# Modulation granules earlier in the weight stream of a two-layer hybrid decoder trunk

## The chip, the cores and the metric

One core of a Trainium2 chip. The metric is the device time of one execution in microseconds (us). The kernel before takes 1177.0 us, the median of three runs from 1176.92 to 1178.7. PE is TensorE, DVE is VectorE, ACT is ScalarE, POOL is GpSimd and SP is SyncE, which issues the loads.

## The reference

Two layers over one sequence of 256 rows and 1024 channels, all in float32. Each layer has three parts: a SwiGLU network (FFN1), token mixing, and another SwiGLU network (FFN2). Each part starts with a normalisation whose scale and shift, and ends with a residual whose gate, come from a vector c through a 1024 x 9216 matrix per layer:

```python
def modulate(x, g, shift, scale):
    return rmsnorm(x, g) * (1 + scale[:, None, :]) + shift[:, None, :]

c_act = jax.nn.silu(c)
for l in range(DEPTH):
    mod = c_act @ w_ada[l] + b_ada[l]
    sh1, sc1, gt1, sh2, sc2, gt2, sh3, sc3, gt3 = jnp.split(mod, N_MOD, axis=-1)
    h = modulate(x, ln_ffn1_g[l], sh1, sc1)
    x = x + 0.5 * gt1[:, None, :] * swiglu(h, ffn1_w_gate[l], ffn1_w_up[l], ffn1_w_down[l])
    h = modulate(x, ln_mix_g[l], sh2, sc2)
    x = x + gt2[:, None, :] * token_mixing(h, w_in[l], ...)
    h = modulate(x, ln_ffn2_g[l], sh3, sc3)
    x = x + 0.5 * gt3[:, None, :] * swiglu(h, ffn2_w_gate[l], ffn2_w_up[l], ffn2_w_down[l])
return rmsnorm(x, final_g)
```

Token mixing projects h once and feeds three groups of heads: a convolution of 31 taps with a normalisation over channels, block-sparse attention, and a gated delta rule. Their outputs go through one output projection.

## The kernel before, in words

The activations stay on the chip, transposed: xT has 128 partitions, 8 channel blocks and 256 sequence columns. All weights, 252.9 MB of them, are read once from DRAM, in granules of 1 MB (256 columns or 256 rows of a matrix), into a ring of four tiles `raw` (N_RAW = 4). SP issues a granule when the one four places before it has been released, that is, when every unit cut from it has been read. The order of the granules is the list `seq`, written by `plan_ffn` and `plan_mix` before any instruction is.

A weight unit is 128 output columns of all 1024 channels. It is split in two parts for TensorE: ACT writes the rounded part `hi`, then DVE writes the rest `lo` (POOL in the opening, where `cfg["lo_first"]` says "gp"). The activations are split in the same way, and PE adds three products for each of 8 blocks, hi by hi, hi by lo and lo by hi, so 24 products of 256 columns per unit. Six converted units can be waiting (N_UNIT = 6).

A modulation vector v of layer l (0 shift, 1 scale, 2 gate of FFN1; 3 to 5 of mixing; 6 to 8 of FFN2) takes four granules of `w_ada` (`adaunit`). DVE multiplies the rows of each granule by the partition's element of c_act and adds them up, two operations per granule (`ada_step`), in a tile of 128 x 1024 called `Lb` or `adaacc`. `extract` then turns this tile with PE, four transposes at a time into `px`, and sums each turned block with a reduction on DVE into the columns of `mod`; `complete` adds the bias. Biases, gains and convolution taps are loaded as rows (`rowsA`, `rowsB`) and turned into columns by `columns(l, part)`: part 0 the biases, part 1 the other rows, and rowsB, which holds the convolution taps.

The table `ADA` says which vectors are loaded during which part: in layer 0 vectors 2 to 5 in FFN1, 6 and 7 in mixing; in layer 1 vector 7 alone in mixing. `plan_ffn` spreads them over the slots of its loop over pairs of units (`extra`). `plan_mix` places a granule behind every fourth converted unit, counting from the second, and puts those that remain behind the last granule of `w_out`.

The opening: scale (vector 1 of layer 0) is loaded first and summed while ACT and PE make the sums of squares. With scale known, xT times scale is split in S-hi (tiles S6a, Q) and S-lo (S3a, V, v), and six units are multiplied with it, without shift. Shift (vector 0) is loaded behind the second gate granule. When its sum is there, `columns(0, 1)` and the extraction follow, and the part that shift adds to the six units is made by 96 row products (`sh_b`), turned at the end (`turn_row`) and used as a bias. The following units use H, the full modulated input. At the starts of the other parts the shift instead stands in two more columns of S6a to v, so that products of 258 columns bring its part along.

In mixing the order of instructions comes from a planner: the class `Clock` keeps an estimated time for each engine, and the code asks it before it converts a unit (`pump`), extracts a vector, or gives a convolution tap to DVE (`cacc` from `hc` and `colB`) or to ACT and POOL (`ctap`, then `cacc`). One recurrence on POOL inverts small matrices; its result goes through DRAM (`scr_w`) into `Wc`.

Of the kernel before, what the change touches and what calls it, by code (L numbers as in the profile page):

```python
# [11 lines left out]
F32R = mybir.dt.float32r  # L12
# [165 lines left out]
def trunk(ctx, tc, t, out):  # L178
# [121 lines left out]
    def plan_ffn(l, which, ada):  # L300
# [11 lines left out]
        start = 4 if key == ("f", 0, 1) else 0  # L312
# [8 lines left out]
        for q in range(FB // 2):  # L321
            for n, w in (("g", wg), ("u", wu)):
                g = kgran(w, 256 * q, 256)
                for j in range(2):
                    wunit(key + (n, 2 * q + j), g, kview(256, j))
                if key == ("f", 0, 1) and (q, n) == (1, "g"):
                    for i in range(4):
                        adaunit(0, 0, i)
            if q:
                extra(2 * q - 2)  # L330
                for j in range(2):
                    down(2 * q - 2 + j)
                extra(2 * q - 1)
# [4 lines left out]
    def plan_mix(l, ada):  # L338
# [5 lines left out]
        def unit(name, i, g, view, width=D):  # L344
# [4 lines left out]
            if todo and count[0] >= count[1]:  # L349
                adaunit(*todo.pop(0))  # L350
                count[1] += 4
# [57 lines left out]
    for i in range(4):  # L409
        adaunit(0, 1, i)  # L410
# [44 lines left out]
    def extract():  # L455
# [18 lines left out]
        if (l, v) == (1, 0):  # L474
            columns(l, 1)
# [3 lines left out]

    def ada_step(item):  # L480
        _, (l, v), g, i, _ = item
        raw = grans[g]["tile"].rearrange("p (k n) -> p k n", n=D)
        if i == 0:
# [185 lines left out]
    def begin(gs, sh):  # L669
# [4 lines left out]
        if sh is not None:  # L674
# [3 lines left out]
        return dict(gs=gs, sh=sh, parts=[(a[:, :S1 if sh is not None else S], b[:, :S1 if sh is not None else S])  # L678
                                         for a, b in zip(his, los)])
# [95 lines left out]


    scr_g = nc.dram_tensor("scr_g", [D], F32, kind="Internal").ap()

    def ffn(l, which, G, normed, gate_v, nxt):
# [4 lines left out]
        def act_fn(f, o):  # L784
            if bias and f < 4:
                s = normed_out(o[:, 0])
                act.activation(s, s, AF.Silu, bias=bias[2 + f])
            else:
                s = sb([128, S], "tmp2", bufs=4)
                act.activation(s, o[:, 0], AF.Silu)  # L790
# [107 lines left out]
        def first():  # L898
            keys = [key + (n, i) for n in "gu" for i in range(2)]
            if G["sh"] is not None:  # L900
                cols = [sb([128, 2], f"bias{i}") for i in range(2)]
                outs = [bank((128, S1)) for _ in range(2)] + [ps([128, S1], f"a{i}") for i in range(2)]
                norm = {}
                first_units(keys, outs, G, lambda: norm.update(h=normed([pump] * 3)))
                for i in range(2):
                    for j in range(2):
                        dve.tensor_copy(cols[i][:, j:j + 1], outs[2 * j + i][:, S:S + 1])
            else:
                keys += [key + ("g", i) for i in (2, 3)]
                pair = [ps([128, 2, S], f"a{i}") for i in range(2)]  # L910
                raws.extend(bank() for _ in range(2))
                outs = [pair[i][:, j] for j in range(2) for i in range(2)] + [o[:, 0] for o in raws]
                for kk, o in zip(keys, outs):
                    low_last(o, need(kk), G["parts"])
                for k in range(KB):
                    act.activation(nscr["t"][:, k], xT[:, k], AF.Copy, scale=G["gs"][:, k:k + 1])
                    gp.tensor_tensor(nscr["t"][:, k], nscr["t"][:, k], nscr["r"], op=OP.mult)
                while (0, 0) not in ada_acc or not ada_wait:
                    step_stream()
                both = sb([128, KB, 2], "sh_b", F32R)  # L920
                p = [ps([2, n, 128], tag) for n, tag in ((4, "a2"), (2, "m0"))]
                job = ada_wait[0]
                columns(0, 1)
                keep_warm(3)
                for h in range(2):
                    extract()
                    c = slice(4 * h, 4 * h + 4)
                    act.copy(both[:, c, 0], job[3][:, c])
                    dve.tensor_tensor(both[:, c, 1], job[3][:, c], both[:, c, 0], op=OP.subtract)
                for h in range(2):  # L930
                    for i, kk in enumerate(keys):
                        for k in range(4 * h, 4 * h + 4):
                            for x, w in enumerate(conv[kk]):
                                mm(p[i // 4][:, i % 4], both[:, k], w[:, k], k == 0 and x == 0 and i % 4 == 0, (k, x) == (KB - 1, 1))
                row = sb([2, 6, 128], "Wc")
                early = {}

                def rows_out():
                    act.copy(row[:, 0:4], p[0])
                    act.copy(row[:, 4:6], p[1])  # L940

                norm = dict(h=normed([lambda: None] * 3 + [lambda: [done(kk, 1, True) for kk in keys[:2]]], True))
                rows_out()
                early.update((i, normed_out(outs[i])) for i in range(4))
                act.preload_act_table_set("silu_and_others")
                for i, kk in enumerate(keys[2:]):
                    done(kk, 2 * (i == 3), True)

                def turn_row():
                    p = ps([128, 6, 2], "a3")  # L950
# [1045 lines left out]
```

## Time and profile before

| | |
|---|---|
| median of three runs | 1177.0 us |
| profiled execution | 1178.1 us, span 1176.3 us |
| PE busy | 1103.2 us (94%) |
| DVE busy | 875.1 us (74%) |
| ACT busy | 597.3 us (51%) |
| POOL busy | 141.9 us (12%) |
| mean granted clock of PE | 0.978 |
| DMA | 256.52 MB, mean 218 GB/s |
| opening, up to the first down product of FFN1 | 0 to 70 us |
| FFN1, mixing, FFN2 of layer 0 | to about 235, 424 and 600 us |

The span runs from the first to the last instruction; the 1.8 us between it and the execution's own time lie around it. The kernel's instructions all go through one helper, so they carry the line L171, and groups are told apart by the tiles that they write and read. A row "out<-in" names them without buffer numbers. In a timeline the number in square brackets is how long the engine stood idle before the row, and behind the arrow is what ended it. Matmuls overlap one another, so the distance between starts says what one costs. An f32 product takes two rows; a split product (hi, lo) takes one.

### The profile page before, as it was taken

The numbers are of one execution on the slowest core, as the hardware profiler recorded it, in microseconds if no ns is written. First come the engines' busy times: TensorE is split into PE (matmuls) and PEld (weight loads), VectorE is DVE, ScalarE is ACT, GpSimd is POOL, SyncE is SP. The second block draws the span as 40 slices with busy tenths as digits, with TensorE's granted clock in tenths as the row PEclk, the third lists the DMA queues.
The fourth block names the chain that finished last, engine by engine and source line by source line (L and its number), as shares of the span: only waits on it lengthen the run. The fifth ranks groups of instructions, "written<-read, shape, count | busy, mean of one in ns | idle before, by whom it ended". The sixth has DMA issues, their size and how long they took to land.

```text
span 1176.3 us, 22000 instructions
## 1 busy us (share of the span) xinstructions
PE 1103.2 (94%) x9085; PEld 1037.8 (88%) x9085; DVE 875.1 (74%) x1350; ACT 597.3 (51%) x1011; POOL 141.9 (12%) x187
## 2 busy tenths in 40 slices
PE   5799999999969689999999999999996999999997
PEld 4799999968868689999999999997785899999996
DVE  5778778757977788867779887774877869766554
ACT  4364444448356464534456444444764676544443
POOL 0710000020650010000001000001037101000002
PEclk9899999999989999999999999999998999999999
DMA  9759798846423558968864997882562434876640
GB/s 327 251 171 345 282 335 279 265 123 198 125 100 131 186 173 298 329 237 318 287 228 159 333 331 254 306 287 80 166 202 75 145 102 157 310 239 216 208 132 36
DMA packets 167660, 256.52 MB, mean 218 GB/s; under 512 B 8272, under 2 KB 134056, under 8 KB 167560
## 3 DMA queue, kind: packets, MB, share of 16 engines
q1 hardware_dynamic: 166536, 252.95, 63.5%
q0 software_dynamic: 1024, 2.16, 0.8%
q8 instruction: 71, 1.16, 0.4%
q14 instruction: 29, 0.24, 0.1%
HBM read 252.86 MB, written 2.23 MB: 217 GB/s over the span
## 4 chain that ended last, share of the span: by engine, by line
PE 74%; DVE 10%; ACT 7%; POOL 4%; issue 2%; DMA 2%; SPq 0%; POOLq 0%; ACTq 0%; DVEq 0%
PE pm L171 45%; PE pa L171 26%; DVE adaacc L171 3%; PE px L171 2%; DVE lo L171 2%; ACT hi L171 1%; ACT tmp L171 1%; ACT L171 1%; POOL xin_LT L171 1%; DMA raw<-in_w_in_dram 1%; DVE S3a L171 1%; DVE mod L171 1%; POOL W L171 1%; DMA xin_LT<-in_x_dram 1%; DVE v L171 1%
## 5 line engine op out<-in xcount | busy, mean ns | idle before, releaser
L171 PE MATMUL pm<-H,hi 128*128 128x256 f32 x2816 | 510.0, 283 | 1.2 <-DVE H L171 1.2
L171 DVE TENSOR_TENSOR lo<-raw,hi 128x1024 fp32r<-128x1024 f32 (+1 forms) x300 | 361.3, 1227 | 110.9 <-ACT hi L171 110.4
L171 PEld LDWEIGHTS pm<-H,hi 128*128 128x128 f32 x2816 | 433.7, 190 | 4.3 <-DVE H L171 1.4
L171 ACT CAST hi<-raw 128x1024 fp32r<-128x1024 f32 (+1 forms) x306 | 311.5, 1042 | 193.1 <-PE pm L171 84.2
L171 PE MATMUL pm<-H,lo 128*128 128x256 f32 x1408 | 393.0, 281 | 0.0
L171 PEld LDWEIGHTS pm<-H,lo 128*128 128x128 f32 x1408 | 265.4, 189 | 0.0
L171 PE MATMUL pa<-Y,hi 128*128 128x256 f32 x1312 | 236.3, 283 | 3.7 <-DVE xT L171 3.7
L171 PEld LDWEIGHTS pa<-Y,hi 128*128 128x128 f32 x1312 | 202.6, 191 | 4.3 <-DVE xT L171 4.3
L171 PE MATMUL pa<-Y,lo 128*128 128x256 f32 x656 | 184.6, 281 | 0.0
L171 PEld LDWEIGHTS pa<-Y,lo 128*128 128x128 f32 x656 | 126.3, 193 | 0.0
L171 POOL TENSOR_TENSOR xin_LT<-xin_LT 128x256 f32<-128x256 f32 x35 | 27.2, 776 | 645.0 <-ACT xin_LT L171 642.7
L171 ACT CAST Y<-tmp 128x256 fp32r<-128x256 f32 x88 | 35.8, 406 | 120.4 <-DVE tmp L171 120.4
L171 DVE SCALAR_TENSOR_TENSOR adaacc<-raw,c_act,adaacc 128x1024 f32<-128x1024 f32 x70 | 93.9, 1342 | 1.6
L171 DVE SCALAR_TENSOR_TENSOR Lb<-raw,c_act,Lb 128x1024 f32<-128x1024 f32 x56 | 71.8, 1282 | 4.3 <-DMA raw<-in_w_ada_dram 3.0
L171 DVE TENSOR_TENSOR Y<-tmp,Y 128x256 fp32r<-128x256 f32 x88 | 37.4, 425 | 41.6 <-ACT Y L171 41.6
L171 PE MATMUL pm<-Y,raw 128*128 128x256 f32 x288 | 65.9, 382 | 0.0
L171 PEld LDWEIGHTS pm<-Y,raw 128*128 128x128 f32 x288 | 53.6, 190 | 7.5
L171 PE MATMUL pa<-hi,Y 128*128 128x512 f32 x176 | 54.8, 393 | 0.0
L171 ACT ACTIVATE tmp<-pm 128x256 f32<-128x256 f32 x78 | 29.6, 379 | 49.4 <-PE pm L171 49.3
L171 DVE TENSOR_REDUCE mod<-px 128x4 f32<-128x512 f32 x34 | 23.5, 690 | 38.5 <-PE px L171 38.4
L171 DVE SCALAR_TENSOR_TENSOR cacc<-hc,colB,cacc 128x256 f32<-128x256 f32 x92 | 44.7, 499 | 4.6 <-POOL cacc L171 3.1
L171 DVE TENSOR_TENSOR tmp<-tmp,pm 128x256 f32<-128x256 f32 x80 | 33.2, 415 | 12.1 <-ACT tmp L171 12.1
(302 smaller groups left out, 1278.3 us busy)
## 6 DMA issues: line engine op xcount, KB each, us to landing
raw<-in_w_ada_dram SPq DMA_DIRECT2D x70, 1024.0 KB
raw<-in_ffn_w_gate_dram SPq DMA_DIRECT2D x44, 1024.0 KB
raw<-in_ffn_w_up_dram SPq DMA_DIRECT2D x44, 1024.0 KB
raw<-in_ffn_w_down_dram SPq DMA_DIRECT2D x44, 1024.0 KB
raw<-in_w_in_dram SPq DMA_DIRECT2D x12, 1024.0 KB
raw<-in_w_in_dram SPq DMA_DIRECT2D x20, 512.0 KB
raw<-in_w_out_dram SPq DMA_DIRECT2D x16, 512.0 KB
raw<-in_w_in_dram SPq DMA_DIRECT2D x4, 768.0 KB
```

What stands on the lines that cost most here:

```text
L171: return getattr(real, op)(*args, **kw)
```

## The change

1. In the opening, the four granules of shift are loaded directly behind those of scale. DVE sums only the first half of the rows of each granule; the other half goes to PE as f32 products of c_act with the raw rows, 512 columns at a time, and two more products with ones add the 128 partial sums of DVE (`ada_rows`). Two copies, eight transposes of one column each and a copy give the vector. Four units are computed with 258 columns, instead of six without shift; the 96 row products, two groups of warming products and `turn_row` fall away. xT times scale times rstd (PT) is made by eight operations of DVE, before by ACT and POOL. POOL makes two lo, before six.
2. `plan_ffn` starts placing the modulation granules of the first FFN1 at slot 2, before at slot 4.
3. `plan_mix` places a modulation granule behind every second converted unit, before every fourth.
4. `columns(0, 1)`, which turns rowsB, comes behind the extraction of vector 2 in FFN1, before in the opening.

The core of the diff (three hunks that only rename or drop the old opening are cut):

```diff
-        start = 4 if key == ("f", 0, 1) else 0
+        start = 2 if key == ("f", 0, 1) else 0
...
-                if key == ("f", 0, 1) and (q, n) == (1, "g"):
-                    for i in range(4):
-                        adaunit(0, 0, i)
...
                 adaunit(*todo.pop(0))
-                count[1] += 4
+                count[1] += 2
...
-    for i in range(4):
-        adaunit(0, 1, i)
+    for v in (1, 0):
+        for i in range(4):
+            adaunit(0, v, i)
...
-        if (l, v) == (1, 0):
+        if (l, v) in ((0, 2), (1, 0)):
             columns(l, 1)
...
+    def ada_rows(raw, g, i):
+        if i == 0:
+            ada_acc[0, 0] = [ps([1, 512], f"a{2 + h}") for h in range(2)] + [sb([128, D], "adaacc")]
+        *rows, acc = ada_acc[0, 0]
+        halves = [slice(512 * h, 512 * h + 512) for h in range(2)]
+        for h in range(2):
+            mm(rows[h], c_act[:, 2 * i + 1:2 * i + 2], raw[:, 1, halves[h]], i == 0, False)
+        c = c_act[:, 2 * i:2 * i + 1]
+        if i == 0:
+            dve.tensor_scalar(acc, raw[:, 0], c, 0.0, op0=OP.mult, op1=OP.add)
+        else:
+            dve.scalar_tensor_tensor(acc, raw[:, 0], c, acc, op0=OP.mult, op1=OP.add)
+        release(g)
+        if i < 3:
+            return
+        row = sb([1, D], "Lb")
+        for h in range(2):
+            mm(rows[h], ones[:, 0:1], acc[:, halves[h]], False)
+            dve.tensor_copy(row[:, halves[h]], rows[h])
+        p = ps([128, KB], "x")
+        for k in range(KB):
+            pe.transpose(p[:, k:k + 1], row[:, 128 * k:128 * k + 128], ident[0:1, 0:1])
...
+    def first_serial(keys, outs, G, between):
+        for i, (key, o) in enumerate(zip(keys, outs)):
+            low_last(o, need(key), G["parts"], between if i == 0 else None)
...
     gs = need_mod(0, 1)
     G = begin(gs, None)
-    keep_warm(3)
+    rstd(sums)
     for k in range(KB):
         scaled_hi(G, k)
-        scaled_lo(G, k)
-    step_stream()
-    rstd(sums)
-    for _ in range(4):
+    for i in range(4):
+        step_stream()
+        for k in {1: range(4), 2: range(4, KB)}.get(i, ()):
+            scaled_lo(G, k)
+    cfg["lo_first"] = ["gp", "gp"]
+    G["sh"] = mods[0, 0]
+    for _ in range(2):
+        step_stream()
+    G["shift"](G["sh"])
+    for k in range(KB):
+        dve.scalar_tensor_tensor(nscr["t"][:, k], xT[:, k], gs[:, k:k + 1], nscr["r"], op0=OP.mult, op1=OP.mult)
+    for _ in range(2):
         step_stream()
```

The program of DVE in the opening, behind the scale of layer 0 (mod_174 is scale, mod_253 shift; `lo` are weight units), as it is now:

```order
L171 TENSOR_SCALAR adaacc<-raw,c_act 128x1024
L171 SCALAR_TENSOR_TENSOR adaacc<-raw,c_act,adaacc 128x1024
L171 SCALAR_TENSOR_TENSOR S3a<-xT,mod_174,S6a 128x256 x3
L171 SCALAR_TENSOR_TENSOR V<-xT,mod_174,S6a 128x256
L171 SCALAR_TENSOR_TENSOR adaacc<-raw,c_act,adaacc 128x1024
L171 SCALAR_TENSOR_TENSOR V<-xT,mod_174,S6a 128x256 x2
L171 SCALAR_TENSOR_TENSOR v<-xT,mod_174,Q_192 128x256 x2
L171 SCALAR_TENSOR_TENSOR adaacc<-raw,c_act,adaacc 128x1024
L171 COPY Lb<-pa_206 1x512
L171 COPY Lb<-pa_207 1x512
L171 COPY mod_253<-px 128x8
L171 TENSOR_TENSOR mod_253<-mod_253,colA 128x8
```

Before, the sum of shift (adaacc) stood behind all S-lo pieces and two lo, as one block of eight operations; now it is four operations, and the first units' shift columns follow directly.

SP's program at the end of mixing 0 (raw is the ring; `w_out` is the output projection's weight, `ffn_w_gate` the first of FFN2), before:

```order
L171 DMA raw<-in_w_in_dram 128x8x256
L171 DMA raw<-in_w_in_dram 128x8x128
L171 DMA raw<-in_w_in_dram 128x4x384 x2
L171 DMA raw<-in_w_ada_dram 128x2x1024
L171 DMA raw<-in_w_in_dram 128x8x256
L171 DMA raw<-in_w_in_dram 128x8x128
L171 DMA raw<-in_w_out_dram 128x1024 x8
L171 DMA raw<-in_w_ada_dram 128x2x1024 x5
L171 DMA raw<-in_ffn_w_gate_dram 128x8x256
```

and now:

```order
L171 DMA raw<-in_w_in_dram 128x4x384
L171 DMA raw<-in_w_ada_dram 128x2x1024
L171 DMA raw<-in_w_in_dram 128x4x384
L171 DMA raw<-in_w_ada_dram 128x2x1024
L171 DMA raw<-in_w_in_dram 128x8x256
L171 DMA raw<-in_w_ada_dram 128x2x1024
L171 DMA raw<-in_w_in_dram 128x8x128
L171 DMA raw<-in_w_out_dram 128x1024 x8
L171 DMA raw<-in_w_ada_dram 128x2x1024 x2
L171 DMA raw<-in_ffn_w_gate_dram 128x8x256
```

Five modulation granules stood between the last `w_out` and FFN2's first weight, now two; the other three stand among the granules of `w_in`. In layer 1 it was one and is none.

DVE's program in the same place (mod_4275 is vector 6, shift, and mod_4346 vector 7, scale, of FFN2; xT is the residual), before:

```order
L171 TENSOR_TENSOR lo<-raw,hi 128x1024 x2
L171 SCALAR_TENSOR_TENSOR adaacc<-raw,c_act,adaacc 128x1024 x2
L171 TENSOR_REDUCE mod_4275<-px 128x4 x2
L171 TENSOR_TENSOR mod_4275<-mod_4275,colA 128x8
L171 TENSOR_SCALAR adaacc<-raw,c_act 128x1024
L171 SCALAR_TENSOR_TENSOR adaacc<-raw,c_act,adaacc 128x1024 x7
L171 TENSOR_REDUCE mod_4346<-px 128x4 x2
L171 TENSOR_TENSOR mod_4346<-mod_4346,colA 128x8
L171 SCALAR_TENSOR_TENSOR mod_4346<-mod_4346,colA 128x8
L171 TENSOR_TENSOR sh_l<-mod_4275,sh_h 128x8
```

and now (mod_4272 is vector 7):

```order
L171 TENSOR_TENSOR lo<-raw,hi 128x1024 x2
L171 SCALAR_TENSOR_TENSOR adaacc<-raw,c_act,adaacc 128x1024 x4
L171 TENSOR_TENSOR lo<-raw,hi 128x1024 x3
L171 TENSOR_REDUCE mod_4272<-px 128x4 x2
L171 TENSOR_TENSOR mod_4272<-mod_4272,colA 128x8
L171 SCALAR_TENSOR_TENSOR mod_4272<-mod_4272,colA 128x8
L171 TENSOR_TENSOR sh_l<-mod_3349,sh_h 128x8
```

Vector 6 is finished earlier, inside mixing, and four operations of vector 7's sum are left where ten stood.

## Rows read from the trace of the kernel before

**Rows 1.** Page, part 1: engine, busy us (share of the span), instructions.
```profile
PE 1103.2 (94%) x9085; PEld 1037.8 (88%) x9085; DVE 875.1 (74%) x1350; ACT 597.3 (51%) x1011; POOL 141.9 (12%) x187
```

**Rows 2.** Waits of PE, 65 to 430 us: total, times, longest.
```profile
PE px L171 <- DVE adaacc L171: 8.4, 2, 4.8
PE pa L171 <- DMA Wc<-scr_w: 6.4, 1, 6.4
```

**Rows 3.** Timeline of PE, opening: start us, us, engine line op out<-in xcount [idle before <-releaser].
```profile
25.84 1.11 PE L171 MATMUL pa<-S6a,hi 128*128 128x256 f32 x6
...
43.83 0.23 PE L171 MATMUL px<-kc,rowsA 23*128 23x23 f32 x1
49.90 0.43 PE L171 MATMUL px<-kc,rowsB 98*128 98x98 f32 x1 [5.84 <-DVE colA L171]
...
70.33 0.40 PE L171 MATMUL pa<-Y,hi 128*128 128x256 f32 x2
```

**Rows 4.** Timeline of SyncE's queue, opening.
```profile
11.82 0.40 SPq L171 DMA_DIRECT2D raw<-in_ffn_w_gate_dram  x1
...
20.76 1.08 SPq L171 DMA_DIRECT2D raw<-in_w_ada_dram  x1
```

**Rows 5.** Timeline of DVE, opening.
```profile
24.88 1.27 DVE L171 SCALAR_TENSOR_TENSOR S3a<-xT,mod,S6a 128x256 fp32r<-128x256 f32 x3
...
36.42 13.33 DVE L171 SCALAR_TENSOR_TENSOR adaacc<-raw,c_act,adaacc 128x1024 f32<-128x1024 f32 x7
```

**Rows 6.** Windows: stretch, busy us of each engine (x), PEclk, DMA share, GB/s.
```profile
50.00:54.00 4.00, 4.00 (x13) 3.35 (x14) 0.43 (x2) 0.00 (x0) 1.02 (x2) 0.50 1.09 348
```

**Rows 7.** Timelines of ACT, DVE and POOL, opening.
```profile
20.24 1.04 ACT L171 CAST hi<-raw 128x1024 fp32r<-128x1024 f32 x1 [2.85 <-DMA raw<-in_ffn_w_gate_dram]
...
61.49 2.60 DVE L171 SCALAR_TENSOR_TENSOR H<-PT,mod,H 128x256 fp32r<-128x256 f32 x1
...
61.34 2.46 POOL L171 TENSOR_TENSOR lo<-raw,hi 128x1024 fp32r<-128x1024 f32 x1 [10.32 <-ACT hi L171]
```

**Rows 8.** Page, part 5: op out<-in xcount | busy, mean ns | idle before.
```profile
L171 PE MATMUL pm<-Y,raw 128*128 128x256 f32 x288 | 65.9, 382 | 0.0
```

**Rows 9.** Timeline of DVE, end of mixing 0.
```profile
386.87 0.69 DVE L171 TENSOR_TENSOR Y<-cacc,Y 128x512 fp32r<-128x512 f32 x1 [2.84 <-ACT Y L171]
...
395.54 2.60 DVE L171 SCALAR_TENSOR_TENSOR adaacc<-raw,c_act,adaacc 128x1024 f32<-128x1024 f32 x2
...
416.08 4.63 DVE L171 TENSOR_TENSOR lo<-raw,hi 128x1024 fp32r<-128x1024 f32 x4
```

**Rows 10.** Timeline of PE, end of mixing 0.
```profile
411.61 1.08 PE L171 MATMUL px<-kc,adaacc 128*128 128x128 f32 x4 [4.81 <-DVE adaacc L171]
...
424.23 0.28 PE L171 MATMUL pm<-S6a,hi 128*128 128x258 f32 x1
```

**Rows 11.** Timeline of PE, turns in FFN2 of layer 0.
```profile
523.48 0.29 PE L171 MATMUL px<-kc,rowsA 80*128 80x80 f32 x1 [0.79 <-DVE mod L171]
...
526.26 0.63 PE L171 MATMUL pm<-H,hi 128*128 128x256 f32 x2
```

**Rows 12.** Convolution tile cacc in mixing 0: duration ns min/median/max, first and last start.
```profile
L171 POOL TENSOR_TENSOR cacc<-cacc,ctap x14: 716/734/1536, 328.1 to 362.7; 128x256 f32<-128x256 f32 x14
```

**Rows 13.** Timeline of DVE, end of mixing 1.
```profile
957.62 0.69 DVE L171 TENSOR_TENSOR Y<-cacc,Y 128x512 fp32r<-128x512 f32 x1 [2.84 <-ACT Y L171]
```

**Rows 14.** Timeline of PE, end of mixing 1.
```profile
972.96 0.89 PE L171 MATMUL px<-kc,adaacc 128*128 128x128 f32 x4 [2.20 <-DVE mod L171]
973.50 0.78 PE L171 MATMUL pa<-Y,hi 128*128 128x256 f32 x2
...
980.35 0.40 PE L171 MATMUL pa<-Y,hi 128*128 128x256 f32 x2
980.70 0.28 PE L171 MATMUL pm<-S6a,hi 128*128 128x258 f32 x1
```

**Rows 15.** Waits of SyncE's queue, 65 to 395 us.
```profile
SPq L171 <- DVE adaacc L171: 26.7, 9, 11.8
```

More of the change, by code (lines that the diff above doesn't have):

```diff
@@ L482, in ada_step @@
         raw = grans[g]["tile"].rearrange("p (k n) -> p k n", n=D)
+        if (l, v) == (0, 0):
+            return ada_rows(raw, g, i)
         if i == 0:
@@ L673, in begin, with shift @@
         los = [pieces[2][:, k] for k in range(3)] + [pieces[3][:, k] for k in range(3)] + [pieces[4][:, k] for k in range(2)]
-        if sh is not None:
+        def shift(sh):
             hi, lo = split_col(sh)
@@ L677, in begin @@
                 dve.tensor_copy(pieces[piece][:, :, S:S1], src[:, k:k + n].unsqueeze(2).to_broadcast([128, n, S1 - S]))
-        return dict(gs=gs, sh=sh, parts=[(a[:, :S1 if sh is not None else S], b[:, :S1 if sh is not None else S])
-                                         for a, b in zip(his, los)])
+        if sh is not None:
+            shift(sh)
+        return dict(gs=gs, sh=sh, parts=list(zip(his, los)), shift=shift)
     def begin_whole(gs, sh, w):
@@ L899, in first @@
             keys = [key + (n, i) for n in "gu" for i in range(2)]
[L900 to L918, printed above, removed]
-                    step_stream()
[L920 to L923, printed above, removed]
-                keep_warm(3)
[L925 to L950, printed above, removed]
-                    for i in range(6):
-                        pe.transpose(p[:, i], row[:, i], ident[0:2, 0:2])
-                    b = sb([128, 6], "bias0")
-                    dve.tensor_reduce(b, p, axis=AX.X, op=OP.add)
-                    bias.extend(b[:, i:i + 1] for i in range(6))
-                    acc.extend(ps([128, 2, S], f"a{i}") for i in range(4))
-                    for i in range(2):
-                        first_act(i, early[i], early[2 + i], bias[i], bias[2 + i])
@@ L960, in first @@
-            if G["sh"] is not None:
-                su = [normed_out(o) for o in outs]
-                acc.extend(ps([128, 2, S], f"a{i}") for i in range(4))
-                for kk in keys:
-                    done(kk)
-                act.preload_act_table_set("silu_and_others")
-                for i in range(2):
-                    first_act(i, su[i], su[2 + i], cols[i][:, 0:1], cols[i][:, 1:2])
-                return norm["h"], None
-            return norm["h"], turn_row
-        bias, raws = [], []
@@ L972, in ffn @@
-        hparts, pending = first()
+            cols = [sb([128, 2], f"bias{i}") for i in range(2)]
+            outs = [bank((128, S1)) for _ in range(2)] + [ps([128, S1], f"a{i}") for i in range(2)]
+            norm = {}
+            opening = key == ("f", 0, 1)
+            (first_serial if opening else first_units)(keys, outs, G, lambda: norm.update(h=normed([pump] * 3, opening)))
+            for i in range(2):
+                for j in range(2):
+                    dve.tensor_copy(cols[i][:, j:j + 1], outs[2 * j + i][:, S:S + 1])
@@ L973, in ffn @@
+            su = [normed_out(o) for o in outs]
+            acc.extend(ps([128, 2, S], f"a{i}") for i in range(4))
+            for kk in keys:
+                done(kk)
+            act.preload_act_table_set("silu_and_others")
+            for i in range(2):
+                first_act(i, su[i], su[2 + i], cols[i][:, 0:1], cols[i][:, 1:2])
+            return norm["h"]
+        hparts = first()
         last = list(range(FB - 2 if nxt else FB - 3, FB))
```

28 lines of the change are left out of this document (10 added, 18 removed).

## Prediction

> **What bounds the kernel now.** The page comes first: TensorE (PE) is busy 1103.2 of 1176.3 us [rows 1], so time can only come out of PE's idle stretches or out of stretches where its clock is low. I then asked for PE's waits between 65 and 430 us, which is the rest of FFN1, the first mixing and its end. The largest entry is PE's transposes px waiting for the modulation sums adaacc of VectorE (DVE), 8.4 us in two waits; next come 6.4 us for Wc, the inverse that comes back through DRAM [rows 2]. Third, the timelines of the opening, because that is where PE idles longest. A reader should see there that the first unit starts at 25.84, that six units end at 43.83, that PE then waits 5.84 us for DVE, and that the first down product (the moment when four gate and four up units are done) comes at 70.33 [rows 3]. The wait is DVE's: the four granules of shift are issued behind three weight granules, the first of them at 20.76 [rows 4], and seven operations of their sum take 13.33 [rows 5], where one undisturbed pair takes 2.60 [rows 9]. Behind that wait PE's granted clock is 0.50, that is 1.2 GHz [rows 6]. Last, the two ends of mixing: layer 0 has five trailing modulation granules, layer 1 has one, and the same code otherwise. That comparison carries the largest term.
>
> Gains and losses are sums of differences against the profiled execution, 1178.1 us with its span of 1176.3. The median of the runs shown is 1177.0, so I take differences off that.
>
> **Opening.** The order moves shift's four granules into the ring places of gate, up, gate and the first modulation granule, issued from 11.82 to 20.76 [rows 4]. The first such place landed at 20.24 [rows 7], and at 348 GB/s [rows 6] one MB takes 3.0 us, so the four land at about 20.2, 23.2, 26.2 and 29.2. DVE is done with scale at 24.88, where its S-lo pieces begin [rows 5]; now four half sums stand among eight S-lo operations: 4 x 1.3 (half of the pair of 2.60) and 8 x 0.42 (three take 1.27) give 8.6, so the last half sum ends at 33.5. PE adds the other halves meanwhile; behind DVE remain two f32 products of 512 columns. The kernel has a measured row for f32 products of 256 columns, 65.9 us for 288 rows, two rows per product, so 0.46 each [rows 8]; 512 columns cost 0.92 and the two 1.8, double at the low clock. That makes 35.3. Copies, eight one-column transposes, the sum and the five shift columns follow. The nearest row is the extraction at the end of mixing, from px at 411.61 to the end of its shift columns at 416.08, 4.5 us with wider transposes and two reductions [rows 9, 10]; below it lies 1.5. I take 2.7, nearer the lower end because no reduction (0.69 each) is left. First unit: **38.0** instead of 25.84.
>
> From there PE has no 96 small row products, no warming products and no wait. Six units took 43.83 - 25.84 = 18.0, 3.00 each with the slow start in it [rows 3]. Eight units take 24.0; 1.0 more for the later weights, whose first granule is released by the first shift sum. So the first down product is at 63.0 instead of 70.33: **-7.3**. Best end: first unit at 36.5 and nothing lost behind, -9.8. Worst end: the last products at half clock (1.8) and one small DVE operation blocked by each of POOL's two lo, as one H was for 2.60 beside a lo of POOL [rows 7], where three S-lo pieces of the same size take 1.27 [rows 5]: -2.
>
> The turn of rowsB leaves the opening, where it lay inside the wait, and comes behind the extraction of gate in FFN1. The same three turns stand in FFN2 of layer 0: PE waits 0.79 before the first and then runs slow, two products in 0.63 [rows 11] where 0.40 is usual [rows 3]. Such a slow restart costs 1.6 at the end of mixing 1 (below). So the two turns cost between 0.8 and 2.4, and I take **+1.8**, since the idle time behind which PE restarts is nearly the same. The four vectors of FFN1 that start two slots earlier only spread the loads and sums; DVE has room there, so 0.
>
> **Mixing.** In layer 0 six granules instead of three are summed inside, in layer 1 four instead of three. Each is 2.6 us of DVE and one ring place. PE's idle time inside is set by chains through POOL and DRAM (Wc 6.4), not by DVE's total, and part of the added sum falls in that wait. Thirteen convolution taps move from DVE to POOL (9 and 4), 0.73 each [rows 12]. I take **+1**, between -1 and +8.
>
> The Trainium skill ("SBUF — State Buffer", section "Who interferes with whom") says that a DVE instruction with two SBUF inputs and a GpSimd instruction that reads SBUF exclude each other for a whole instruction. The H row above, 2.60 where a third of 1.27 is usual, agrees. By that rule the thirteen taps could block DVE for their whole length.
>
> **End of mixing 0.** I lay layer 1 over layer 0 by the same DVE row, Y<-cacc at 386.87 and at 957.62, a shift of 570.75 [rows 9, 13]. FFN2 starts at 424.23 in layer 0 and at 980.70 in layer 1 [rows 10, 14]; layer 0 is 424.23 + 570.75 - 980.70 = 14.3 us later, for four more trailing granules. With two left it is layer 1's end and one more pair of 2.60: 14.3 - 2.6 = **-11.7**. The lower bound is three pairs of DVE time, -7.8; the upper -13.
>
> **End of mixing 1.** With none trailing, the 2.20 us wait of px for mod [rows 14] goes, and so does the restart at low clock behind it. The 48 products left then, in 16 steps of three, take 7.2 us from 973.50 to 980.70, and at full clock a step takes 0.35 (980.35 to 980.70), 5.6 in all, so 1.6 goes: **-3.8**, between -2.2 and -4.6. Late next is the chain through the residual to FFN2's first product, which there starts without a wait.
>
> Sum: -7.3 + 1.8 + 1 - 11.7 - 3.8 = -20.0, so 1177.0 - 20.0 = **1157.0**.
>
> **Rivals.**
> - *Mixing gives it back.* The added sums lie on DVE's chain to scr_l and to the lo halves: four granules of 2.6 are 10.4 instead of +1: 1166.4. For it: DVE is busy 74% [rows 1]. Against: PE's large waits there name DMA, not DVE [rows 2]. Chance 0.13.
> - *POOL's taps block DVE.* Thirteen taps of 0.73 [rows 12] hold up two-input operations of DVE, cacc and lo, and PE behind them: 13 x 0.73 = 9.5 instead of +1, 1165.5. Against: fourteen taps in layer 0 at a median of 0.73 put no entry for themselves among PE's waits up to 430 [rows 2, 12]. Chance 0.07. This is the result of the rule named above.
> - *The opening gains nothing.* Four MB ahead of the weights make the first unit later than 45: 1164.3. For it: the four MB land one behind the other, 3.0 us each, before any weight. Chance 0.10.
> - *The trailing sums were not what held FFN2.* Only the DVE time of three pairs goes (-7.8) and mixing 1 gives 2.2: 1162.5. Chance 0.08.
> - *Slower: the ring stalls.* Four raw buffers; a granule of modulation holds one until DVE reaches it. SyncE's queue has waited 26.7 us in nine waits for adaacc, the longest 11.8 [rows 15]. If each of the four moved granules waits the longest and the following weights reach PE late by as much, 4 x 11.8 = 47.2: 1204. It decides from 20 us of new PE waits in mixing, 5 per granule. Against: these nine waits were there already, and none of PE's entries up to 430 names hi, lo or a granule [rows 2]. Chance 0.05.
> - *It does not do what it says*: the earlier places could be given back by the planner, so that the last sums again come behind the output projection. The order shows the trailing issues at two and none, so I leave this at no chance of its own.
>
> **How the numbers follow.** The forecast has 0.57: 1150 (all best ends: -9.8 + 0.8 - 1 - 13 - 4.6 = -27.6) to 1163. The range 1148 to 1168 takes in the next four cases. Outside lie the ring and sums of bad ends. About 0.2%, 2.4 us, is what a measurement of this kernel tells from no change. Slower by more than that: 0.05, the ring; within: 0.02, two bad cases at once; faster: 0.93.
>
> **What would show it.** Right: px<-adaacc gone from PE's waits up to 430 except about 1 us; first unit near 38 and first down product near 63; the distance from Y<-cacc to FFN2's first product falls from 37.4 to 25.7 in layer 0 and from 23.1 to 19.3 in layer 1; the distance from the first down product to Y<-cacc of layer 0 (316.5) longer by about 3. Wrong: a first unit behind 45, new PE waits for hi or lo in mixing, SyncE waits for adaacc above 12 us there, or taps of POOL as releasers of PE.

## The result and the profile after

The kernel after takes 1168.7 us (median of four runs, 1166.5 to 1171.2). The kernel before, run beside it, takes 1177.9. The ratio is 0.992 [0.990, 0.994], so 9.2 us are gained where 20.0 were forecast, and the forecast range ended just below, at 1168. The profiled execution of after took 1166.5 us, span 1164.7, and is the fastest of the four: the stages below add up to 11.6 us and not to 9.2.

The stages, from the starts of the same instructions in the two profiled executions (us):

| stage | before | after | difference | forecast |
|---|---|---|---|---|
| to the first down product | 70.3 | 62.1 | -8.3 | -7.3 |
| rest of FFN1, with the moved turn | 168.3 | 170.2 | +2.0 | +1.8 |
| mixing 0, to Y<-cacc | 148.3 | 151.3 | +3.0 | } +1 |
| mixing 1, to Y<-cacc | 148.6 | 149.3 | +0.7 | } |
| end of mixing 0 | 37.4 | 26.9 | -10.5 | -11.7 |
| end of mixing 1 | 23.1 | 18.5 | -4.6 | -3.8 |
| FFN2 and FFN1 between | 384.8 | 387.1 | +2.3 | 0 |
| last FFN2 and norm | 195.6 | 199.4 | +3.8 | 0 |

The last two rows were in no sum. No product of theirs was touched, yet they lose 6.1 us. (Differences are of the unrounded starts.)

Page of after, part 1 (as [rows 1]):

```profile
PE 1106.5 (95%) x8991; PEld 1030.5 (88%) x8991; DVE 864.1 (74%) x1350; ACT 599.8 (51%) x1013; POOL 131.4 (11%) x188
```

PE has 94 instructions fewer than before and is busy 3.3 us longer. That is the same surprise in one line. The waits of PE in after, 60 to 430 us (as [rows 2]), look as they were forecast: the 8.4 us for adaacc and the 6.4 for Wc are gone, and smaller ones stand there:

```profile
PE pa L171 <- DVE E L171: 3.9, 2, 3.3
PE px L171 <- DVE mod L171: 3.1, 3, 1.8
PE pm L171 <- DMA raw<-in_w_in_dram: 2.8, 1, 2.8
PE pa L171 <- DVE Y L171: 2.8, 1, 2.8
```

Timeline of PE in after, opening (as [rows 3]):

```profile
31.64 1.88 PE L171 MATMUL pa<-adaacc,ones 128*1 128x512 f32 x4 [1.13 <-DVE adaacc L171]
...
37.69 1.63 PE L171 MATMUL pm<-S6a,hi 128*128 128x258 f32 x6 [3.00 <-DVE S3a L171]
...
50.66 0.39 PE L171 MATMUL pm<-H,hi 128*128 128x256 f32 x2
...
62.06 0.40 PE L171 MATMUL pa<-Y,hi 128*128 128x256 f32 x2
```

The first unit starts at 37.69 (forecast 38.0), four units are done at 50.66, and the first down product comes at 62.06 (63.0). Timelines of DVE and POOL in after, opening:

```profile
23.96 0.74 DVE L171 TENSOR_SCALAR adaacc<-raw,c_act 128x1024 f32<-128x1024 f32 x1
...
30.31 1.27 DVE L171 SCALAR_TENSOR_TENSOR adaacc<-raw,c_act,adaacc 128x1024 f32<-128x1024 f32 x1
...
35.41 2.05 DVE L171 TENSOR_TENSOR sh_l<-mod,sh_h 128x8 fp32r<-128x8 f32 x1 [0.26 <-ACT sh_h L171]
...
32.78 4.67 POOL L171 TENSOR_TENSOR lo<-raw,hi 128x1024 fp32r<-128x1024 f32 x2 [32.32 <-ACT hi L171]
```

The last half sum ends at 31.58, 1.9 before the forecast; 0.9 of this comes from scale, which is done at 23.96 here and was done at 24.88 in before [rows 5]. But then the operation sh_l on 8 columns takes 2.05 us while POOL makes its two lo, and ends with POOL's, at about 37.45. This is the small blocked operation that the prediction had only in its worst end.

Timelines of DVE and PE in after, end of mixing 0 (as [rows 9, 10]):

```profile
383.54 0.69 DVE L171 TENSOR_TENSOR Y<-cacc,Y 128x512 fp32r<-128x512 f32 x1 [3.62 <-ACT Y L171]
...
394.23 5.24 DVE L171 SCALAR_TENSOR_TENSOR adaacc<-raw,c_act,adaacc 128x1024 f32<-128x1024 f32 x4
...
401.12 0.60 PE L171 MATMUL px<-kc,adaacc 128*128 128x128 f32 x4
...
403.54 0.66 PE L171 MATMUL px<-kc,adaacc 128*128 128x128 f32 x4 [1.82 <-DVE mod L171]
...
410.41 0.28 PE L171 MATMUL pm<-S6a,hi 128*128 128x258 f32 x1
```

The px transposes no longer wait for the sum. From Y<-cacc to FFN2 it is now 26.9, forecast 25.7. Timeline of PE in after, end of mixing 1 (as [rows 14]):

```profile
962.26 0.51 PE L171 MATMUL pa<-Y,hi 128*128 128x256 f32 x2 [0.80 <-DVE xT L171]
...
965.32 0.28 PE L171 MATMUL pm<-S6a,hi 128*128 128x258 f32 x1
```

### The profile page after: what moved, and what is told of

Its sections match the earlier page's. It is cut to its first block, busy times and chain, and to the rows that moved or that the text cites. A ratio compares the mean times of both kernels' runs of the same rounds, so it can differ in the third digit from the quotient of the medians.

```text
span 1164.7 us, 21807 instructions
## 1 busy us (share of the span) xinstructions
PE 1106.5 (95%) x8991; PEld 1030.5 (88%) x8991; DVE 864.1 (74%) x1350; ACT 599.8 (51%) x1013; POOL 131.4 (11%) x188
## 4 chain that ended last, share of the span: by engine, by line
PE 75%; DVE 11%; ACT 5%; POOL 4%; issue 2%; DMA 2%; SPq 0%; POOLq 0%; DVEq 0%; ACTq 0%
PE pm L171 45%; PE pa L171 28%; DVE lo L171 2%; PE px L171 2%; POOL xin_LT L171 2%; DVE cacc L171 1%; POOL cacc L171 1%; ACT hi L171 1%; DVE S3a L171 1%; ACT tmp L171 1%; DVE adaacc L171 1%; ACT L171 1%; DVE tmp L171 1%; DMA raw<-in_w_in_dram 1%; DVE Y L171 1%
## 5 line engine op out<-in xcount | busy, mean ns | idle before, releaser
L171 PE MATMUL pm<-H,hi 128*128 128x256 f32 x2848 | 519.6, 284 | 0.0
L171 PEld LDWEIGHTS pm<-H,hi 128*128 128x128 f32 x2848 | 440.2, 189 | 2.9 <-issue 1.2
L171 PE MATMUL pm<-H,lo 128*128 128x256 f32 x1424 | 402.4, 283 | 0.0
L171 PEld LDWEIGHTS pm<-H,lo 128*128 128x128 f32 x1424 | 269.2, 189 | 0.0
L171 PEld LDWEIGHTS pa<-Y,lo 128*128 128x128 f32 x656 | 123.8, 189 | 0.0
L171 DVE SCALAR_TENSOR_TENSOR adaacc<-raw,c_act,adaacc 128x1024 f32<-128x1024 f32 x66 | 87.2, 1320 | 1.3
L171 DVE SCALAR_TENSOR_TENSOR Lb<-raw,c_act,Lb 128x1024 f32<-128x1024 f32 x56 | 71.8, 1282 | 4.3 <-DMA raw<-in_w_ada_dram 3.0
L171 DVE TENSOR_TENSOR Y<-tmp,Y 128x256 fp32r<-128x256 f32 x88 | 37.4, 425 | 41.6 <-ACT Y L171 41.6
L171 PEld LDWEIGHTS pm<-Y,raw 128*128 128x128 f32 x288 | 54.7, 194 | 13.5 <-DMA raw<-in_w_in_dram 5.7
L171 DVE SCALAR_TENSOR_TENSOR cacc<-hc,colB,cacc 128x256 f32<-128x256 f32 x79 | 39.8, 515 | 8.8 <-POOL cacc L171 7.5
L171 POOL TENSOR_TENSOR cacc<-cacc,ctap 128x256 f32<-128x256 f32 x41 | 40.9, 1007 | 43.0 <-ACT ctap L171 25.6
```

The costliest lines, as they stand in the source:

```text
L171: return getattr(real, op)(*args, **kw)
```

## The experiments

In all, before was run beside the others at 1178.4 to 1179.0. Intervals are those of the ratio to it.

### Both kernels again, and the parts

`c_before` and `c_after` are the two kernels unchanged. `e_open` is after with the old spacing of mixing, `e_mix` is before with the new one:

```diff
 e_open, in after        e_mix, in before
-count[1] += 2          -count[1] += 4
+count[1] += 4          +count[1] += 2
```

> The kernel before, once more, with a profile on the same chip as the three runs beside it. In the first pair of profiles the stage from FFN2's first product of layer 1 to the end took 195.6 us before and 199.4 after, although the change touches nothing there. Theory A (the pace of PE's products differs from execution to execution, not from kernel to kernel): here too this stage may come out anywhere from 195 to 200, and equal to that of the changed kernel within 1.5 us. Theory B (the changed program slows PE in stages it doesn't touch): 195 to 196 here, 199 or more for the changed kernel. Time 1177 by both.

> The changed kernel, once more. Time 1166 to 1171. By theory A the last stage is within 1.5 us of that of the kernel before in this call, and the difference of the two profiles is the sum of the touched stages (-8.3 opening, +2.0 rest of FFN1, +3.0 and +0.7 in mixing, -10.5 and -4.6 at its ends: -17.7) but for the pace. By theory B the last stage is again 3 to 4 us longer than before.

> The changed kernel with plan_mix placing a granule behind every fourth unit again: opening, start slot and moved turn alone. By the stages: -8.3 + 2.0 = -6.3, so 1171; mixing and its ends as before (37.4 and 23.1 us from Y<-cacc to FFN2's first product). If the opening gave nothing: 1177 to 1179. By theory B its last stage is slow as well, if the slow pace comes with the opening: 1177.

> The kernel before with plan_mix placing a granule behind every second unit: the mixing part alone. By the stages: -10.5 - 4.6 + 3.0 + 0.7 = -11.4, so 1166. If the mixing gave back what its ends gain: 1177. By theory B its last stage is slow, if the slow pace comes with the mixing: 1172.

Measured: c_before 1178.5, 1.000 [0.999, 1.001]; c_after 1169.7, 0.992 [0.991, 0.994]; e_open 1181.1, 1.002 [1.001, 1.003]; e_mix 1169.7, 0.994 [0.992, 0.996].

The opening, the turn and the earlier granules of FFN1 together lose 2.6 us, although the first down product of e_open comes at 61.9, where c_before has 69.3; none of the times expected of e_open was above 1179. The spacing in mixing gives 8.8 alone and 11.4 on top of e_open. So the gain of the opening is given back somewhere. In e_open the FFN stages behind the first down product together take 8.5 us more than in c_before, 10.7 more than in e_mix. In c_after they are longer too, with no new wait in PE's lists, and with a granted clock of 1.00 in the last stage as in c_before. What differs is the pace. The products of the last stage in c_before, by shape (busy us, mean ns):

```profile
L171 PE MATMUL pm<-H,hi 128*128 128x256 f32 x640 | 113.1, 279 | 0.0
...
L171 PE MATMUL pa<-hi,Y 128*128 128x512 f32 x176 | 54.8, 393 | 0.0
```

and in c_after:

```profile
L171 PE MATMUL pm<-H,hi 128*128 128x256 f32 x640 | 115.4, 283 | 0.0
...
L171 PE MATMUL pa<-hi,Y 128*128 128x512 f32 x176 | 55.4, 396 | 0.0
```

The same 640 products take 2.3 us more. Laid out over the program, the mean distance between the starts of two neighbouring products of 256 columns without idle time is 117.0 ns in c_before, 116.8 in e_mix, 118.5 in c_after and 118.4 in e_open. There are some 6,000 such distances, and 6,000 x 1.4 ns is 8.4 us.

### Where the tiles lie

What e_open and after share, and before and e_mix do not, is the order in which tiles are first used. The program gives each tile its SBUF address in this order. In bytes of each partition:

| | hi | lo | Y | H0 | H1 |
|---|---|---|---|---|---|
| before | 96512 | 121088 | 164288 | 181824 | 190016 |
| after | 119296 | 143872 | 168512 | 178816 | 187008 |

The theory was that this placement sets PE's pace; the rival, that the new instructions do. `p_after` is after with the places of before, and `p_before` the reverse: unused tiles of the same names are taken ahead, so that not one instruction differs. More tiles move than the five of the table: those that the list names besides, and what stands behind them.

```diff
 in after (p_after), behind columns(0, 0); in before (p_before) with the order of after
+    for shape, tag, dt, n in (((128, D), "hi", F32R, N_UNIT), ((128, D), "lo", F32R, N_UNIT), ((128, KB), "mod1", F32, 2), ((128, 6, S1), "S6a", F32R, 1),
... (eleven more tiles in p_after; p_before has a list of its own)
+        for _ in range(n):
+            pool.tile(list(shape), dt, name=tag, tag=tag, bufs=n)
```

> The changed kernel with the tiles hi, lo, Y, H0 and H1 placed in SBUF where they lie in the kernel before (96512, 121088, 164288, 181824, 190016 instead of 119296, 143872, 168512, 178816, 187008); the same instructions in the same order. Theory P (PE's pace hangs on where these tiles lie, and the new opening moved them): the last stage goes from 199.5 back to 195.6, and the 6,000 or so products of 256 columns from a mean distance of 118.4 ns to 117.0, which is 8 us over the kernel: 1161 to 1162. Theory O (the pace hangs on something else of the opening, as how PE or its clock starts): last stage 199.5, 1169 to 1170.

> The kernel before with hi, lo, Y, H0 and H1 placed where they lie in the changed kernel; the same instructions. Theory P: last stage 199 instead of 195.6, mean distance 118.4 ns, 1186 to 1187. Theory O: 195.6, 117.0 ns and 1178.

Measured: p_after 1163.3, 0.988 [0.986, 0.989]; p_before 1186.9, 1.007 [1.006, 1.009]. The last stage of p_after, by shape, is that of c_before again:

```profile
L171 PE MATMUL pm<-H,hi 128*128 128x256 f32 x640 | 113.1, 279 | 0.0
```

and p_before has c_after's 115.4 and 283. The mean distances are 117.2 and 118.5. So the places alone cost the change 6.4 us (p_after against c_after), and those of after would cost before 8.4. In before's places the program's change is worth 1178.5 - 1163.3 = 15.2, and in after's 1186.9 - 1169.7 = 17.2.

### What about the places

Within one kernel the pace differs by tile: in before the steps that move Y are 115.9 ns apart, those that move H 117.3 to 117.6; in after 117.4 and 118.7 to 118.9. The moved tile's address less the weight tile's, modulo 256 bytes, is 192 for Y and 64 for H in before, 64 and 128 in after. The next kernels put Y, H0 and H1 in front, with pads:

```diff
 in after, behind columns(0, 0) (p_448)
+            ((128, 48), "pad0", F32, 1),
+            ((128, 2, 5, S), "Y", F32R, 1),
+            ((128, KB, S), "H0", F32R, 1),
+            ((128, KB, S), "H1", F32R, 1),
+            ((128, 16), "pad1", F32, 1),
+            ((128, D), "hi", F32R, N_UNIT),
+            ((128, D), "lo", F32R, N_UNIT),
...
```

`p_256` leaves out both pads, `q_rel0` the second, `q_rel192` the first. `b_448` is before with the block of p_448.

> The changed kernel with Y, H0 and H1 at addresses whose remainder by 1024 is 448 (that of Y in the kernel before, whose products were the fastest, 115.9 ns), hi and lo with the remainder that they have in the changed kernel (512). If the remainder of the moving tile alone sets the pace: all products near 116 ns, 1154 to 1156. If it is the distance between moving and weight tile, or neighbours in the layout, something else: 117 to 119 ns and 1161 to 1172. By theory O: 1169 to 1170.

> The same with all of Y, H0, H1, hi and lo at remainder 256. If the remainder of the moving tile alone sets the pace, a fourth value of it besides 448 (115.9 ns), 576 (117.5) and 640 (118.8); the theory doesn't say which. If the distance between moving and weight tiles sets it, this is distance 0. By theory O: 1169 to 1170.

> The changed kernel with Y, H0, H1 at remainder 192 by 256, as in the 1146.5 us version, and hi and lo at 192 as well (there 0). In all layouts so far hi and lo had remainder 0 by 256, so the moving tile's own remainder and its distance from the weights could not be told apart. If the moving tile's own remainder decides: 114.3 ns between products again and 1146 to 1147. If the distance to the weights (now 0, as in the layout with 119.9 ns) decides: 119.9 ns and 1177.

> The mirror of it: Y, H0, H1 at remainder 0 by 256 (as in the layout with 119.9 ns), hi and lo at 64, so the distance is 192, as in the 1146.5 us version. Own remainder decides: 119.9 ns, 1177. Distance decides: 114.3 ns, 1146 to 1147.

> The kernel before in the layout of the 1146.5 us version (distance 192 by 256 between Y, H0, H1 and hi, lo), nothing else changed. If the layout's worth is the same for both programs: 117.05 ns between products becomes 114.2, 6,050 x 2.85 = 17 us: 1161 to 1162. If the layout helps only where the new opening stands: 1178.

| | Y, H mod 256 | hi, lo mod 256 | distance | ns between starts | us, ratio |
|---|---|---|---|---|---|
| p_448 | 192 | 0 | 192 | 114.3 | 1146.5, 0.973 [0.970, 0.976] |
| b_448 | 192 | 0 | 192 | 113.8 | 1161.4, 0.986 [0.984, 0.987] |
| q_rel192 | 0 | 64 | 192 | 115.8 | 1158.8, 0.983 [0.982, 0.985] |
| p_256 | 0 | 0 | 0 | 119.9 | 1177.4, 0.999 [0.998, 1.000] |
| q_rel0 | 192 | 192 | 0 | 119.9 | 1176.4, 0.999 [0.998, 1.000] |

q_rel0 differs from p_448 by 64 bytes in the place of hi, lo and the tiles behind them, and Y and H stay. It is 29.9 us slower. p_256 lacks both pads (192 and 64 bytes), so against p_448 every tile behind them lies 256 bytes lower, and modulo 256 only Y, H0 and H1 have moved; it is 30.8 us slower. p_448 came out faster than any time expected of it. The last stage of p_448, by shape:

```profile
L171 PE MATMUL pm<-H,hi 128*128 128x256 f32 x640 | 110.6, 278 | 0.0
...
L171 PE MATMUL pa<-hi,Y 128*128 128x512 f32 x176 | 54.5, 391 | 0.0
```

and of q_rel0:

```profile
L171 PE MATMUL pm<-H,hi 128*128 128x256 f32 x640 | 116.0, 284 | 0.0
...
L171 PE MATMUL pa<-hi,Y 128*128 128x512 f32 x176 | 54.5, 391 | 0.0
```

The products of 512 columns, in which hi moves and Y is the weights, take the same in both. The others show their pace in single steps of three products, two with the weights hi and one with lo. Timeline of PE in p_448, in FFN1:

```profile
101.10 0.39 PE L171 MATMUL pa<-Y,hi 128*128 128x256 f32 x2
...
101.44 0.39 PE L171 MATMUL pa<-Y,hi 128*128 128x256 f32 x2
```

and in q_rel0:

```profile
101.31 0.40 PE L171 MATMUL pa<-Y,hi 128*128 128x256 f32 x2
...
101.67 0.40 PE L171 MATMUL pa<-Y,hi 128*128 128x256 f32 x2
```

0.34 us a step against 0.36. That the same remainder 0 of hi is best (p_448) and worst (p_256), and the same remainder 192 of Y and H too, excludes that a tile's own place decides; what goes with the pace in all these layouts is the distance. q_rel192, 1.5 ns slower than p_448 at the same distance, shows that something else has a smaller part. b_448 against p_448 gives the change 14.9 us in a third layout, beside 15.2 and 17.2.

Two finer distances, on the kernel `d_nopool` of the next part: `pd_224` (pad1 of 32 bytes) and `pd_160` (96 bytes).

> The fastest version with hi and lo 32 bytes lower, so that the distance of Y, H0 and H1 from them is 224 by 256 instead of 192. Distances so far: 0 gave 119.9 ns between products, 64 117.4 to 117.6, 128 118.8, 192 114.0 to 115.9. If the pace depends on the distance in steps of 64: 114.0 to 115.9 ns, 1143 to 1155. If it runs on between 192 and 0: near 117 ns, 1160.

> The same with hi and lo 32 bytes higher than in the fastest version: distance 160. Steps of 64 from 128: 118.8 ns, 1170; steps of 64 centred on 192: 114 to 116 ns, 1143 to 1155; running on between 128 and 192: near 116.5 ns, 1157.

Measured: pd_224 1169.4, 0.992 [0.990, 0.994], at 118.3 ns, slower than both times expected of it; pd_160 1167.3, 0.992 [0.988, 0.995], at 118.2 ns. Both are 24 to 26 us slower than d_nopool, which has the distance 192. But hi and lo there also start off a multiple of 64 bytes, and which of the two it is wasn't told apart.

### The opening's parts

On p_448, `d_dve` gives DVE both halves of the rows of shift (no row products), and `d_nopool` puts the shift columns ahead of the next two units and gives their lo to DVE instead of POOL:

```diff
 d_dve
-            mm(rows[h], c_act[:, 2 * i + 1:2 * i + 2], raw[:, 1, halves[h]], i == 0, False)
...
+        for j in range(2):
+            c = c_act[:, 2 * i + j:2 * i + j + 1]
+            if i + j == 0:
+                dve.tensor_scalar(acc, raw[:, j], c, 0.0, op0=OP.mult, op1=OP.add)
+            else:
+                dve.scalar_tensor_tensor(acc, raw[:, j], c, acc, op0=OP.mult, op1=OP.add)
...
-            mm(rows[h], ones[:, 0:1], acc[:, halves[h]], False)
+            mm(rows[h], ones[:, 0:1], acc[:, halves[h]], True)
```

```diff
 d_nopool
-    cfg["lo_first"] = ["gp", "gp"]
     G["sh"] = mods[0, 0]
+    G["shift"](G["sh"])
     for _ in range(2):
         step_stream()
-    G["shift"](G["sh"])
```

> The 1146.5 us version with shift's granules summed by VectorE alone (both halves of the rows, eight operations instead of four and eight row products). By the prediction's step the second halves are 4 x 1.3 = 5.2 us on DVE and nothing on PE, so the first unit comes at 43.0 instead of 38.0, and the first down product at 67 to 68 instead of 62.9: 1151 to 1152. Rival: the sum is not on the path (the first weights land at 31.7 and POOL's lo ends at 37.4): first unit unchanged, 1146.5.

> The 1146.5 us version with the shift columns made ahead of the first two units and VectorE making their lo instead of POOL. Theory (POOL's lo blocked sh_l, 2.05 us instead of 0.16): sh_l takes 0.16 again, the first unit comes at 36.3 to 36.5 instead of 38.0, the first down product 1.5 earlier: 1145. Rival: VectorE's two lo (2.4 us) ahead of PT make the third unit late, and the gain is gone: first unit at 36.4, first down product at 62.9 or later, 1146.5 or more.

Measured: d_dve 1152.3, 0.978 [0.976, 0.979]; d_nopool 1143.6, 0.970 [0.968, 0.973]. Against p_448 d_dve is 5.8 us slower. d_nopool is 2.9 faster, but its four runs (1141.1 to 1147.1) and those of p_448 (1142.8 to 1149.3) overlap, so this is no measured price of POOL's two lo. In the two traces 2.3 of the difference lie in the rest of FFN1 (163.8 against 166.0), where neither edit stands and the products are 113.4 ns apart in d_nopool and 115.2 in p_448, in the same places. Timeline of DVE in d_dve, opening:

```profile
33.76 5.11 DVE L171 SCALAR_TENSOR_TENSOR V<-xT,mod,S6a 128x256 fp32r<-128x256 f32 x2
```

and of POOL in the same kernel:

```profile
33.76 4.82 POOL L171 TENSOR_TENSOR lo<-raw,hi 128x1024 fp32r<-128x1024 f32 x2 [33.30 <-ACT hi L171]
```

Two pieces of S-lo, 0.42 each by [rows 5], last as long as the two lo of POOL beside them. So the first unit of d_dve, at 47.7 where 43.0 was expected, and its first down product, at 71.8, hold more than the sums, and the 5.8 us are not the price of the sums alone. Timeline of DVE in d_nopool:

```profile
36.48 0.17 DVE L171 TENSOR_TENSOR sh_l<-mod,sh_h 128x8 fp32r<-128x8 f32 x1 [0.26 <-ACT sh_h L171]
```

Without POOL's lo sh_l takes 0.17, where after has 2.05. From the vector of shift (mod with its bias) to the first unit it is 1.4 us in d_nopool and 3.3 in p_448; in d_nopool the first unit then waits for ACT's hi. The Trainium skill ("SBUF — State Buffer", section "Who interferes with whom") has such pairs of DVE and GpSimd exclude each other for a whole instruction, and the two pairs of rows agree. d_nopool has the lowest median here, 25 us below after.

### The spacing in mixing

On d_nopool, `m_4` and `m_3` place a granule behind every fourth and every third unit:

```diff
 m_4                     m_3
-count[1] += 2          -count[1] += 2
+count[1] += 4          +count[1] += 3
```

> The fastest version so far (1143.6 us) with plan_mix placing a granule behind every fourth unit again. By the prediction's terms the denser placing is worth 11.7 + 3.8 - 1 = 14.5 us: 1158. If the mixing gives back 5.7 of it, as the stages of the changed kernel in the layout of before have it (+2.3 and +3.4 inside mixing, -10.1 and -4.6 at its ends): 1152 to 1153. If the mixing gives nearly all back: 1144 to 1146.

> The fastest version with a granule behind every third unit: four inside mixing of layer 0 instead of six, four trailing. If the gain lies at the end of mixing 0 alone (2.6 us for each trailing granule and a px wait): 5 to 7 us slower, 1149 to 1151, layer 1 unchanged. If the sums inside mixing cost as much as at its end: 1143 to 1145.

Measured: m_4 1151.0, 0.976 [0.974, 0.978]; m_3 1161.5, 0.985 [0.983, 0.988]. The spacing is worth 7.4 us, half of the 14.5 that the terms of mixing and its two ends give. By stages, d_nopool gains 10.6 and 3.7 at the two ends and loses 4.4 and 1.3 inside.

Inside, the convolution is late. With three granules more to sum, the planner gives POOL 23 taps in mixing 0 instead of 14. Tile cacc in mixing 0 of after (as [rows 12]):

```profile
L171 POOL TENSOR_TENSOR cacc<-cacc,ctap x23: 720/1068/1724, 316.8 to 358.4; 128x256 f32<-128x256 f32 x23
```

Their median is 1,068 ns, not 734. DVE starts its last tap at 360.9 in d_nopool and at 349.7 in m_4, and Y<-cacc comes at 377.9 against 371.8. PE then waits 2.8 for Y, in d_nopool as in after (the list of waits above), a wait that neither before nor m_4 has. Which of the taps on POOL, the sums on DVE and the low clock delays the rest was not separated.

The ring is not it. Waits of SyncE's queue in after, 60 to 395 us (as [rows 15]):

```profile
SPq L171 <- DVE adaacc L171: 30.3, 11, 8.7
```

3.6 us more than before, and the longest is 8.7, not 11.8; of PE's waits one of 2.8 names a granule.

m_3 was a miss: it was to lie between d_nopool and m_4, or at d_nopool, and it is 10.5 us slower than m_4. Its ends take 39.8 and 29.2, longer than either's (26.9 and 18.5; 37.5 and 22.2). Mixing 0 and its end together take 185.6 as in m_4; the loss is in mixing 1 and its end, 182.2 against 172.7. There PE waits 4.0 for tmp of ACT, which it doesn't in m_4, and the granted clock is 0.50 for 6.8 us from within that wait; why was not followed up.

## Why the prediction was wrong

The forecast was -20.0; in c_after against c_before it is -8.8. Of the 11.2 us between them the places of the tiles make 6.4: in before's places the change takes 1163.3, inside the range. There (p_after against c_before, profiled executions) the steps can be read without the pace:

| step | forecast | measured in before's places |
|---|---|---|
| opening | -7.3 | -7.0 |
| moved turn | +1.8 | +0.3 (all of the rest of FFN1) |
| mixing, both | +1 | +5.6 (2.2 and 3.4) |
| end of mixing 0 | -11.7 | -10.2 |
| end of mixing 1 | -3.8 | -4.5 |
| everything else | 0 | 0.0 (-0.6 and +0.5) |
| sum | -20.0 | -15.8 (medians -15.2) |
| places of hi, lo, Y and H | no term | +6.4 (medians) |

**The step that failed** is a term that the sum lacked. "Gains and losses are sums of differences against the profiled execution": five terms for the touched places, and so every product that was not touched kept the price of before. The sum gave 0 to some 750 us of FFN. The new order of first uses moved Y from distance 192 to 64 and H from 64 to 128 of the weights, and some 6,000 products came 1.4 ns later behind the one before them. That the places cost this is shown: p_after and p_before change places and no instruction. That it is the places of hi, lo, Y and H, and not of a tile that moves with them, rests on p_448, p_256 and q_rel0 and on the products that are slowed, which read these tiles. No rival of the prediction named it, and none of its views could price it, since before has each tile in one place. That Y and H had different paces in before was in its trace, though: 115.9 against 117.3 to 117.6.

**Mis-sized: mixing.** +1 was taken, +5.6 came in before's places, inside the range of -1 to +8. Two executions of one kernel differ here, by 1.1 us in mixing 1 for before and c_before, by 1.5 for after and c_after, so the size is rough. The first two rivals had the direction right, and neither its size (+10.4 and +9.5): the gain at the ends is partly given back inside. The wait for Wc went, and E, Y and a granule took its place. But PE's waits inside mixing 0 did not grow: they total 13.5 us in c_before, 11.6 in c_after and 13.1 in p_after. What grew from c_before to c_after is PE's busy time there, from 134.5 to 137.6 us, at a mean granted clock of 0.97 and 0.95; how much of it is the clock was not separated. So in mixing 0 the price was not in PE's waits, where the prediction looked for it. In median the spacing was worth 7.4 to 11.4 in three surroundings.

**Right: the opening**, by two errors that cancel, which is luck. The half sums ended 1.9 us early, the blocked sh_l cost 1.9 (2.05 against 0.17), and the first unit came 0.3 before its forecast. The rival "gains nothing" fell.

**Right by chance: the turn.** After's profile shows +2.0 in the rest of FFN1 where +1.8 was forecast, and c_after's +1.8. p_after shows +0.3 there: 1.5 of it is the pace. A term that agrees in one trace isn't thereby shown.

**Right: the ends**, 26.9 and 18.5 against 25.7 and 19.3. The rival that only DVE's -7.8 goes fell. That the ring stalls fell too: 30.3 us of waits, nothing near 47 more.

## What to carry to other kernels

When the same products of an untouched stage take a different mean time after an edit, compare the addresses of their operands before looking for a cause in the edit: an earlier first use of one tile moved every later one. To price an edit, run it also with the old places (unused tiles of the same names, taken in the old order). And shift the places on purpose once: here 64 bytes were worth 30 us, three times the change itself.

## What was not expected of the hardware

**Pace by distance.** By the distance of the two SBUF addresses of a split product of 256 columns modulo 256 the mean distance between starts is 119.9 ns at 0, 117.3 to 117.6 at 64, 118.7 to 118.9 at 128 and 113.8 to 115.9 at 192; the two runs off a multiple of 64 have 118.2 and 118.3. The Trainium skill ("SBUF — State Buffer", section "Who interferes with whom") gives PE two independent read ports of SBUF, one for the moved operand and one for weight loads. If the two were independent of each other's addresses as well, the 64 bytes between p_448 and q_rel0 would change nothing; 29.9 us were measured, and the measurement decides. What makes the difference inside the chip was not found out. It does not carry over to every shape of this kernel: the products of 512 columns take 54.5 us in p_448 and in q_rel0, and the rows of the f32 products pm<-Y,raw start 215.8 ns apart in c_before, c_after, p_448 and q_rel0 alike.

**A low clock that differs between executions.** In mixing the granted clock is at 1.2 GHz in some stretches, and which these are isn't the same for every execution. Windows of after (us busy of each engine with counts, then PEclk, DMA share, GB/s):

```profile
310.00:316.00 6.00, 4.59 (x41) 4.24 (x37) 5.93 (x11) 1.72 (x3) 5.78 (x6) 1.00 0.05 8
320.90:323.70 2.80, 2.80 (x15) 2.80 (x15) 2.80 (x6) 0.74 (x2) 2.80 (x3) 0.50 1.07 309
```

and of c_after, the same program:

```profile
310.00:316.00 6.00, 5.09 (x43) 4.61 (x40) 5.93 (x12) 1.73 (x3) 5.76 (x6) 1.00 0.12 16
320.90:323.70 2.80, 2.80 (x26) 2.80 (x25) 2.77 (x7) 1.51 (x3) 2.80 (x3) 1.00 1.08 356
```

In both PE stands idle for a part of the first window and is busy all the time in the second, with 15 products at 0.50 and 26 at 1.00. The longest such stretch is in e_mix:

```profile
364.00:381.00 17.00, 17.00 (x82) 14.34 (x82) 9.37 (x26) 3.38 (x10) 0.40 (x1) 0.50 0.00 0
```

This execution of e_mix took 1174.4 where its median is 1169.7, so a stage of mixing in one trace is good to some 5 us only.
